# Hybrid decoder step on one core: the y products of eight heads in one burst, four buffers for the cumulative sums, a 4 KB DMA scratch

## The chip, the cores and the metric

The kernel runs on one core of a Trainium2 chip. The core has five engines with a queue each: TensorE (PE, matrix products), VectorE (DVE), ScalarE (ACT), GpSimd (POOL) and SyncE (SP, which here issues most DMAs). An engine works through its own queue in order; a wait at the head holds what is behind it. Sixteen DMA engines serve all queues. The metric is the device time of one execution in microseconds.

## The reference

One layer of a hybrid decoder on 256 prompt tokens and 8 x 8 sample tokens (320 in all), model width 2048, float32:

```python
h = rms_norm(x, p["norm_mix_pre"])
proj = h @ p["w_in"]                       # gate u, v; z; x, B, C; dt
gate_out, chunk_v = chunk_spatial_gate(a_u, a_v, ...)
ssm_out, new_ssm, new_ssm_conv = ssd_mixer(z, xbc, dt_raw, ...)
mix = jnp.concatenate([gate_out, ssm_out], axis=-1) @ p["w_out"]
x = x + rms_norm(mix, p["norm_mix_post"])
f, new_ffn_conv = conv_ffn(rms_norm(x, p["norm_ffn_pre"]), ...)
x = x + rms_norm(f, p["norm_ffn_post"])
```

The change lies in the chunked scan of `ssd_mixer`, which has 32 heads in 4 groups:

```python
seg = da_cs[:, :, :, None] - da_cs[:, :, None, :]
decay = jnp.exp(jnp.where(mask, seg, -jnp.inf))
cb = jnp.einsum("bctgn,bcsgn->bctsg", cc, bc)
y_diag = jnp.einsum("bctsgr,bcsgrp->bctgrp", cb[..., None] * decay, xdt)
...
y_off = jnp.einsum("bctgn,bcgrpn,bctgr->bctgrp", cc, states_in, jnp.exp(da_cs))
```

`da_cs` are the cumulative sums of dt times a. For each head the decay matrix is made from them, multiplied by `cb`, and then multiplied with the inputs of that head: that is the y product.

## The kernel before

All 320 tokens are kept as columns. A weight matrix comes in slabs of 128 x 1024 values: `slab` (L118) asks for one through SP into a `wraw` buffer (three of them), ACT casts it to a high part `whi` (L128), and DVE subtracts to get the low part `wlo` (L130); each of these has three buffers too. `accumulate` (L139) then runs three products of 128 x 128 weights on 128 x 320 columns (L141, L142, L143): high x high, high x low, low x high. A slab holds eight such weight blocks, so 24 products. `project` (L166) computes 512 output columns of a projection that way, `chunk_out` (L222) adds 512 rows of an output projection to `acc`.

Work that is not weight products is written as generators ("tasks") in the list `bg`; `tick` (L154) runs the first task to its next `yield`. `project` and `chunk_out` call `tick` after a slab, once or `rate` times, so the number of `yield`s sets how far along the weight stream a step stands in program order. That is not the final order: at the end a scheduler places every engine's instructions by priority (program order, moved by `high_priority` and `issue_after`) and by when it thinks their inputs and buffers are there, and can pull a ready instruction ahead of its place.

The scan of a group is the task `ssd(g)` (L767). In order: transposes of x to token order (`xt_ps`), state loads, the loads of the cumulative sums (`load_sums`, L780: two heads' sums, broadcast to 128 partitions, 320 KB, into a `cs` buffer), the chunk's state (`s1_ps`), `cb` (`cb_ps`) and the sample states' part (`yo_ps`). Then for each head `decays(hl)` (L874). For the first head of a pair: ACT takes the exponential of the sums (L880) into `cpx`, POOL multiplies by C (L881). For every head: DVE subtracts (L887, three instructions), ACT takes the exponential (L889), DVE multiplies by `cb` (L891), all in place in `cs`. `products(j)` (L894) runs the products of a pair of heads into one PSUM tile `y_ps` (L902) and DVE adds the skip term into `xs` (L912). After all of them POOL scales the state (L924), `final()` (L927) multiplies the last state product (`fin_ps`, L929) and DVE adds it (L931). The small PSUM tiles (`misc`, L57: `y_ps`, `fin_ps`, `xt_ps`, `cb_ps` and others) share a pool of four banks.

Before, the loads of three pairs are asked for together (L830), and `decays` and `products` run in two halves of four heads (L915 to L923); the fourth pair's sums are asked for behind the first half's products, when a `cs` buffer has been read.

`heads_out(g)` (L944) projects z for the group, and its evacuation `z_evac` (L949) multiplies silu(z) into y (`ev` L359 by DVE, silu L360 by ACT), so it needs that group's y. The stream around the four groups is `chunk_out(w_out, 3)`, then for each group the z projection, the next x projection and `chunk_out(w_out, 4 + g)`, with two ticks a slab in most of them (L980 to L999).

[...]

Of the kernel before, what the change touches and what calls it, by code (L numbers as in the profile page):

```python
# [9 lines left out]
F32 = mybir.dt.float32  # L10
# [7 lines left out]
P = 128  # L18
# [3 lines left out]
NT = NP + NS  # L22
# [12 lines left out]
def hybrid_step(  # L35
# [9 lines left out]
    nc = tc.nc  # L45
# [6 lines left out]
    wp = ctx.enter_context(tc.tile_pool(name="wp", bufs=3))  # L52
# [4 lines left out]
    def misc(name):  # L57
        return ms.tile([P, 512], F32, tag="ms", name=name)
# [54 lines left out]
    def turn():  # L113
        return tc.issue_after(in_turn[-1]) if in_turn else nullcontext()

    first_raw = []

    def slab(src):  # L118
        n = src.shape[2]
        with tc.high_priority(offset=100000):  # L120
            m = n * src.shape[1]
            raw = wp.tile([P, 1024], F32, tag="wraw", name="wraw", bufs=3) if len(first_raw) < 2 else first_raw.pop(0)
            with turn() if first_raw else nullcontext():
                slab_load.append(sp.dma_start(raw[:, :m].rearrange("p (a n) -> p a n", n=n), src).ins)
            if first_raw:
                in_turn.append(slab_load[-1])
            hi = wp.tile([P, 1024], F32R, tag="whi", name="whi", bufs=3)
            act.copy(hi[:, :m], raw[:, :m])  # L128
            lo = wp.tile([P, 1024], F32R, tag="wlo", name="wlo", bufs=3)
            dve.tensor_tensor(out=lo[:, :m], in0=raw[:, :m], in1=hi[:, :m].bitcast(F32), op=ALU.subtract)  # L130

        def block(k, c):
            o = k * n + c * P
            return hi[:, o:o + P], lo[:, o:o + P]
        return block
# [30 lines left out]
    def project(w, c0, evac, width=512, late=None, before=None, quiet=0, ready=None, small=0, after=None, ahead=1, rate=1, more=None, held=None):  # L166
# [6 lines left out]
        def part(src, k0, nk, js):  # L173
            wb = slab(src)
            for c, j in enumerate(js):
                for k in range(nk):
                    kt = k0 + k
                    accumulate(ps[j][:, :NT], wb(k, c), hT[0][:, kt, :], hT[1][:, kt, :], kt == 0, kt == KD - 1)
                if kt == KD - 1 and late is None:
                    if before and j in (0, 2):  # L180
                        before()
                    if before and j == 2:
                        for i in range(2):
                            evac(i, ps[i])
                    if not before or j > 1:
                        evac(j, ps[j])
            if k0 < KD - quiet:
                for _ in range(rate):
                    tick()
# [32 lines left out]
    def chunk_out(w, ck, hi, lo, begins, done=None, rate=1):  # L222

        for nb in range(KD):
            if nb % 2 == 0:
                wb = slab(rows_of(w, 4 * ck, 4, P * nb, 256))
            ps = mm.tile([P, 512], F32, tag="mm", name=f"pd_{ck}_{nb}")
            for k in range(4):
                made = accumulate(ps[:, :NT], wb(k, nb % 2), hi[:, k, :], lo[:, k, :], k == 0, k == 3)
            with first():  # L230
                if begins:
                    act.copy(acc[:, nb, :], ps[:, :NT])
                else:
                    dve.tensor_tensor(out=acc[:, nb, :], in0=acc[:, nb, :], in1=ps[:, :NT], op=ALU.add)  # L234
            if done is not None:
                done(nb)
            if nb % 2 == 1:
                for _ in range(rate):
                    tick()
        pd_last.append(made)  # L240
# [141 lines left out]
    def by_head(ap):  # L382
        return ap.rearrange("p (h d) -> p h d", d=64)
# [7 lines left out]
    with ExitStack() as mctx:  # L391
# [350 lines left out]
        with tc.tile_pool(name="sd", bufs=1) as sd:  # L742
# [24 lines left out]
            def ssd(g):  # L767
# [11 lines left out]

                def load_sums(j):  # L780

                    cs = sd.tile([P, 2, NT], F32, tag="cs", name="cs", bufs=3)
                    o = NS * (j // 2)
                    sp.dma_start(cs, dacs_d[h0 + 2 * j:h0 + 2 * j + 2, o:o + NT].unsqueeze(0).broadcast_to([P, 2, NT]))
                    return cs
# [31 lines left out]
                def decayed(i, c):  # L817
                    xde = sd.tile([P, 512], F32, tag="xde", name="xde", bufs=1)
                    pool.tensor_tensor(out=by_head(xde), in0=by_head(xdt[:, c, :]),
                                      in1=dec[:, i, h0:h0 + 8].unsqueeze(2).to_broadcast([P, 8, 64]), op=ALU.mult)  # L820
                    return xde
# [5 lines left out]
                                      op=ALU.mult)  # L827
                sts.append(load_state(3))
                yield from repeat(None, 5)
                sums_of = {j: load_sums(j) for j in range(3)}  # L830
                yield
                ps = misc("s1_ps")
                pe.matmul(ps, btok[:, 0, bs], x0d, start=True, stop=True)
# [36 lines left out]
                def places(hl):  # L870

                    return ((NS, P), (NS + P, P), (0, NS)) if hl < 4 else ((0, P), (P, P), (NP, NS))

                def decays(hl):  # L874
                    j, i = hl // 2, hl % 2
                    at = places(hl)
                    if i == 0:
                        cs = sums_of.pop(j)
                        cpx = sd.tile([P, 2, P], F32, tag="cpx", name="cpx", bufs=2)
                        act.activation(cpx, cs[:, :, at[1][0]:at[1][0] + P], AF.Exp)  # L880
                        pool.tensor_tensor(out=cpx, in0=cpx, in1=cT[:, g, P:2 * P].unsqueeze(1).to_broadcast([P, 2, P]),  # L881
                                           op=ALU.mult)
                    else:
                        cs, cpx = made[hl - 1][1:]
                    m = cs[:, i]
                    for c, (o, n) in enumerate(at):
                        dve.tensor_scalar(out=m[:, o:o + n], in0=m[:, o:o + n], scalar1=nda[:, c, h0 + hl:h0 + hl + 1],  # L887
                                          scalar2=0.0, op0=ALU.add, op1=ALU.min)
                    act.activation(m, m, AF.Exp)  # L889
                    o = NS * (hl // 4)  # L890
                    dve.tensor_tensor(out=m, in0=m, in1=cb[:, o:o + NT], op=ALU.mult)  # L891
                    made[hl] = m, cs, cpx

                def products(j):  # L894

                    ps = misc("y_ps")
                    pair = [(i, *made[2 * j + i]) for i in range(2)]

                    def both(cols, w, x, **flags):
                        for i, m, _, cpx in pair:  # L900
                            hl = 2 * j + i
                            pe.matmul(ps[64 * i:64 * i + 64, cols], w(hl), x(hl, m, cpx), tile_position=(0, 64 * i), **flags)  # L902

                    def hs(hl):
                        return slice(64 * hl, 64 * hl + 64)
                    c0, c1, sm = (slice(o, o + n) for o, n in places(2 * j))
                    both(slice(0, P), lambda hl: xdt[:, 0, hs(hl)], lambda hl, m, cpx: m[:, c0], start=True, stop=True)
                    both(slice(P, NP), lambda hl: xdt[:, 1, hs(hl)], lambda hl, m, cpx: m[:, c1], start=True, stop=False)
                    both(slice(P, NP), lambda hl: s1[:, hs(hl)], lambda hl, m, cpx: cpx[:, hl % 2, :], start=False, stop=True)
                    both(slice(NP, NT), lambda hl: xdt[:, 2, hs(hl)], lambda hl, m, cpx: m[:, sm], start=True, stop=True)  # L910
                    y = xs[:, j, :]
                    dve.scalar_tensor_tensor(out=y, in0=y, scalar=d_col[:, 4 * g + j:4 * g + j + 1], in1=ps[:, :NT],  # L912
                                             op0=ALU.mult, op1=ALU.add)
                x1d = decayed(1, 1)
                for j in range(0, 4, 2):  # L915
                    for hl in range(2 * j, 2 * j + 4):
                        decays(hl)
                        yield
                    yield
                    products(j)  # L920
                    products(j + 1)
                    if j == 0:
                        sums_of[3] = load_sums(3)  # L923
                pool.tensor_tensor(out=by_head(s1), in0=by_head(s1),  # L924
                                   in1=dec[:, 2, h0:h0 + 8].unsqueeze(2).to_broadcast([P, 8, 64]), op=ALU.mult)

# [9 lines left out]
                else:  # L936
                    for _ in final():
                        pass
                    yield

            tasks = [ssd(g) for g in range(4)]
            res = [[] for _ in range(4)]

# [439 lines left out]
```

## Time and profile before

| | us |
|---|---|
| median of 3 runs | 1777.94 (1777.39 to 1778.95) |
| the profiled execution | 1777.77 |
| its span | 1775.7 |
| PE busy in the span | 1766.8 |
| weight load (PEld) busy | 1743.1 |
| DVE busy | 1184.3 |
| ACT busy | 798.8 |
| POOL busy | 273.2 |

The span is the time from the first to the last instruction of the profiled execution; 2.1 us of its time lie around it. Busy times are sums over instructions; matmuls are pipelined, so neighbouring ones overlap in the record and a busy PE can still lose time between two kinds of product. In a row of instructions in time, the columns are start, duration, engine, line, operation, output and inputs, shapes, count, and in brackets the idle time before it and what ended it. The four groups' scans lie between about 430 and 720 us, the FFN from about 820 us on.

### The profile page before, as it was taken

The numbers are of one execution on the slowest core, as the hardware profiler recorded it, in microseconds if no ns is written. First come the engines' busy times: TensorE is split into PE (matmuls) and PEld (weight loads), VectorE is DVE, ScalarE is ACT, GpSimd is POOL, SyncE is SP. The second block draws the span as 40 slices with busy tenths as digits, with TensorE's granted clock in tenths as the row PEclk, the third lists the DMA queues.
The fourth block names the chain that finished last, engine by engine and source line by source line (L and its number), as shares of the span: only waits on it lengthen the run. The fifth ranks groups of instructions, "written<-read, shape, count | busy, mean of one in ns | idle before, by whom it ended". The sixth has DMA issues, their size and how long they took to land.

```text
span 1775.7 us, 31251 instructions
## 1 busy us (share of the span) xinstructions
PE 1766.8 (100%) x12234; PEld 1743.1 (98%) x12234; DVE 1184.3 (67%) x2055; ACT 798.8 (45%) x1108; POOL 273.2 (15%) x591
## 2 busy tenths in 40 slices
PE   9999999999999999999999999999999999999998
PEld 9999999999999899999999999999999999999998
DVE  7348854656877778577966666766666575656475
ACT  7344544333545454445645434343434343433335
POOL 2003210000211101012322212021101010101004
PEclk9999999999999999999999999999999999999999
DMA  7455644445664644444556656566554444444442
GB/s 253 136 165 167 196 151 149 155 154 192 214 211 156 193 161 148 155 161 155 161 189 199 208 174 206 181 197 204 178 194 147 153 150 151 157 146 153 152 149 107
DMA packets 228498, 303.04 MB, mean 171 GB/s; under 512 B 19488, under 2 KB 150656, under 8 KB 228160
## 3 DMA queue, kind: packets, MB, share of 16 engines
q1 hardware_dynamic: 216560, 281.27, 49.5%
q10 hardware_dynamic: 10304, 15.30, 2.4%
q0 software_dynamic: 1488, 4.49, 0.8%
q8 instruction: 96, 1.57, 0.3%
q14 instruction: 50, 0.41, 0.1%
HBM read 283.44 MB, written 17.58 MB: 170 GB/s over the span
## 4 chain that ended last, share of the span: by engine, by line
PE 96%; DVE 1%; DMA 1%; ACT 1%; issue 0%; POOL 0%; SPq 0%; DVEq 0%; ACTq 0%; POOLq 0%
PE ps L141 20%; PE ps L143 20%; PE ps L142 20%; PE pd L141 10%; PE pd L142 10%; PE pd L143 10%; PE y_ps L902 1%; DMA cs<-dacs_d 1%; PE sg L708 0%; PE yo_ps L851 0%; PE up_ps L1197 0%; DMA wraw<-in_w_in 0%; PE tsum L282 0%; PE vt_ps L597 0%; PE xt_ps L380 0%
## 5 line engine op out<-in xcount | busy, mean ns | idle before, releaser
L130 DVE TENSOR_TENSOR wlo<-wraw,whi 128x1024 fp32r<-128x1024 f32 x470 | 584.6, 1244 | 384.7 <-ACT whi L128 382.0
L128 ACT CAST whi<-wraw 128x1024 fp32r<-128x1024 f32 x470 | 492.1, 1048 | 706.1 <-PE ps L142 413.4
L141 PE MATMUL ps<-h_hi,whi 128*128 128x320 f32 x2528 | 783.2, 310 | 1.3 <-DVE ev L359 0.9
L142 PE MATMUL ps<-h_lo,whi 128*128 128x320 f32 x2528 | 780.1, 309 | 0.0
L143 PE MATMUL ps<-h_hi,wlo 128*128 128x320 f32 x2528 | 779.7, 309 | 0.2 <-DVE wlo L130 0.2
L141 PEld LDWEIGHTS ps<-h_hi,whi 128*128 128x128 f32 x2528 | 474.8, 188 | 4.2 <-issue 1.8
L142 PEld LDWEIGHTS ps<-h_lo,whi 128*128 128x128 f32 x2528 | 474.9, 188 | 1.2 <-issue 0.5
L143 PEld LDWEIGHTS ps<-h_hi,wlo 128*128 128x128 f32 x2528 | 474.4, 188 | 0.6 <-DVE wlo L130 0.5
L141 PE MATMUL pd<-fhi,whi 128*128 128x320 f32 x704 | 217.3, 309 | 0.0
L143 PE MATMUL pd<-fhi,wlo 128*128 128x320 f32 x704 | 217.3, 309 | 0.0
L142 PE MATMUL pd<-flo,whi 128*128 128x320 f32 x704 | 217.3, 309 | 0.0
L141 PE MATMUL pd<-ohi,whi 128*128 128x320 f32 x448 | 139.1, 311 | 0.0
L142 PE MATMUL pd<-olo,whi 128*128 128x320 f32 x448 | 139.0, 310 | 0.0
L143 PE MATMUL pd<-ohi,wlo 128*128 128x320 f32 x448 | 138.7, 310 | 0.0
L142 PEld LDWEIGHTS pd<-flo,whi 128*128 128x128 f32 x704 | 132.2, 188 | 0.7
L143 PEld LDWEIGHTS pd<-fhi,wlo 128*128 128x128 f32 x704 | 132.2, 188 | 0.0
L141 PEld LDWEIGHTS pd<-fhi,whi 128*128 128x128 f32 x704 | 132.2, 188 | 0.0
L234 DVE TENSOR_TENSOR acc_ffn<-acc_ffn,pd 128x320 f32<-128x320 f32 x160 | 77.2, 483 | 33.3 <-PE pd L143 32.4
L141 PEld LDWEIGHTS pd<-ohi,whi 128*128 128x128 f32 x448 | 84.1, 188 | 1.0 <-issue 0.4
L142 PEld LDWEIGHTS pd<-olo,whi 128*128 128x128 f32 x448 | 84.1, 188 | 0.7 <-issue 0.4
L143 PEld LDWEIGHTS pd<-ohi,wlo 128*128 128x128 f32 x448 | 84.1, 188 | 0.2 <-issue 0.2
L1094 POOL COPY ptf<-pad 128x2 f32<-128x2 f32 x88 | 19.8, 227 | 405.2 <-DVE pad L1082 404.6
(300 smaller groups left out, 1578.6 us busy)
## 6 DMA issues: line engine op xcount, KB each, us to landing
wraw<-in_ffn_w_up SPq DMA_DIRECT2D x176, 512.0 KB, 3.5
wraw<-in_w_in SPq DMA_DIRECT2D x142, 512.0 KB, 3.5
wraw<-in_ffn_w_down SPq DMA_DIRECT2D x88, 512.0 KB, 3.3
wraw<-in_w_out SPq DMA_DIRECT2D x64, 512.0 KB, 3.3
st<-in_state_ssm SPq DMA_DIRECT2D x64, 256.0 KB, 4.3
out_ssm_state_sample<-st ACTq DMA_DIRECT2D x32, 256.0 KB, 2.6
cs<-dacs_d SPq DMA_DIRECT2D x16, 320.0 KB, 4.9
xr<-in_xT SPq DMA_DIRECT2D x4, 640.0 KB, 4.6
```

The costliest lines, as they stand in the source:

```text
L128: act.copy(hi[:, :m], raw[:, :m])
L130: dve.tensor_tensor(out=lo[:, :m], in0=raw[:, :m], in1=hi[:, :m].bitcast(F32), op=ALU.subtract)
L141: pe.matmul(ps, whi, xhi, start=first, stop=False)
L142: pe.matmul(ps, whi, xlo, start=False, stop=False)
L143: newest[0] = pe.matmul(ps, wlo, xhi, start=False, stop=last).ins
L234: dve.tensor_tensor(out=acc[:, nb, :], in0=acc[:, nb, :], in1=ps[:, :NT], op=ALU.add)
L902: pe.matmul(ps[64 * i:64 * i + 64, cols], w(hl), x(hl, m, cpx), tile_position=(0, 64 * i), **flags)
L1094: pool.tensor_copy(ptf[:, k, :], pad[:, 256:258])
```

## The change

The task asks for all four pairs' sums together, into four `cs` buffers in place of three; it runs the decays of all eight heads, and then the products of all four pairs in one go. One `yield` a group falls away. `cpx` has four buffers in place of two and `wraw` four in place of three. [...]

```diff
-            raw = wp.tile([P, 1024], F32, tag="wraw", name="wraw", bufs=3) if len(first_raw) < 2 else first_raw.pop(0)
+            raw = wp.tile([P, 1024], F32, tag="wraw", name="wraw", bufs=4) if len(first_raw) < 2 else first_raw.pop(0)
...
-                    cs = sd.tile([P, 2, NT], F32, tag="cs", name="cs", bufs=3)
+                    cs = sd.tile([P, 2, NT], F32, tag="cs", name="cs", bufs=4)
...
-                sums_of = {j: load_sums(j) for j in range(3)}
+                sums_of = {j: load_sums(j) for j in range(4)}
...
-                        cpx = sd.tile([P, 2, P], F32, tag="cpx", name="cpx", bufs=2)
+                        cpx = sd.tile([P, 2, P], F32, tag="cpx", name="cpx", bufs=4)
...
-                for j in range(0, 4, 2):
-                    for hl in range(2 * j, 2 * j + 4):
-                        decays(hl)
-                        yield
+                for hl in range(8):
+                    decays(hl)
                     yield
+                yield
+                for j in range(4):
                     products(j)
-                    products(j + 1)
-                    if j == 0:
-                        sums_of[3] = load_sums(3)
...
-    nc = _bacc.Bacc("TRN2", target_bir_lowering=False, num_devices=1)
+    nc = _bacc.Bacc("TRN2", target_bir_lowering=False, num_devices=1, dynamic_dma_scratch_size=4096)
```

## The prediction

> **What bounds the kernel now.** I read the page's first lines and the chain that ended last, then the busy time by stage, then the order of TensorE's (PE's) instructions around the products of y.
>
> ```profile
> span 1775.7 us, 31251 instructions
> PE 1766.8 (100%) x12234; PEld 1743.1 (98%) x12234; DVE 1184.3 (67%) x2055; ACT 798.8 (45%) x1108; POOL 273.2 (15%) x591
> PE 96%; DVE 1%; DMA 1%; ACT 1%; issue 0%; POOL 0%; SPq 0%; DVEq 0%; ACTq 0%; POOLq 0%
> ...
> 500.00:600.00 100.00, 99.58 (x741) 93.57 (x740) 78.20 (x153) 49.29 (x71) 12.60 (x25) 1.00 0.54 175
> 600.00:720.00 120.00, 118.15 (x888) 113.11 (x889) 85.24 (x170) 54.95 (x79) 13.69 (x20) 1.00 0.51 164
> 830.00:1700.00 870.00, 870.00 (x5917) 868.61 (x5916) 567.00 (x919) 369.76 (x485) 145.04 (x378) 1.00 0.54 174
> ...
> 5.53 6.31 DMA wraw<-in_w_in
> ...
> 813.88 1.23 DVE wlo L130
> ```
>
> The columns of the stage rows are: stretch, its length, then busy time and instructions of PE, weight load, DVE, ACT, POOL, the granted clock, the DMA share and GB/s. The last two rows are of the chain of waits: start, length, what. PE is idle for 1775.7 - 1766.8 = 8.9 us. Of these 0.4 + 1.9 = 2.3 us lie between 500 and 720 us, in the stage of the four ssd groups; nearly all the rest is the start and the tail, where the changed code doesn't run. From 830 to 1700 PE has no gap, so deeper weight loading (the fourth `wraw` buffer) has nothing to win there. What is left is in 436 to 720 us: the idle time, and time in which PE counts as busy while it changes from one kind of product to another.
>
> **The price of a change of kind.** Two full bursts of group 0 and the broken ones of group 1:
>
> ```profile
> 477.49 0.31 PE L143 MATMUL pd<-ohi,wlo 128*128 128x320 f32 x1
> 477.73 0.66 PE L902 MATMUL y_ps<-cs,xdt 128*64 128x128 f32 x8
> ...
> 479.42 0.42 PE L141 MATMUL pd<-ohi,whi 128*128 128x320 f32 x1
> 479.67 0.31 PE L142 MATMUL pd<-olo,whi 128*128 128x320 f32 x1
> ...
> 489.94 0.31 PE L143 MATMUL pd<-ohi,wlo 128*128 128x320 f32 x1
> 490.18 0.66 PE L902 MATMUL y_ps<-cs,xdt 128*64 128x128 f32 x8
> ...
> 492.98 0.31 PE L142 MATMUL ps<-h_lo,whi 128*128 128x320 f32 x1
> ...
> 558.48 0.31 PE L141 MATMUL pd<-ohi,whi 128*128 128x320 f32 x1
> 558.72 0.43 PE L902 MATMUL y_ps<-cs,xdt 128*64 128x128 f32 x2
> 559.08 0.42 PE L142 MATMUL pd<-olo,whi 128*128 128x320 f32 x1
> 559.34 0.31 PE L143 MATMUL pd<-ohi,wlo 128*128 128x320 f32 x1
> ...
> 559.87 0.54 PE L902 MATMUL y_ps<-cs,xdt 128*64 128x128 f32 x5
> ...
> 575.69 0.43 PE L902 MATMUL y_ps<-cs,xdt 128*64 128x128 f32 x2
> ...
> 576.31 0.31 PE L141 MATMUL pd<-ohi,whi 128*128 128x320 f32 x1
> 576.54 0.54 PE L902 MATMUL y_ps<-cs,xdt 128*64 128x128 f32 x5
> ...
> 577.71 0.31 PE L143 MATMUL pd<-ohi,wlo 128*128 128x320 f32 x1
> ...
> 580.50 0.31 PE L141 MATMUL pd<-ohi,whi 128*128 128x320 f32 x1
> 580.74 0.43 PE L902 MATMUL y_ps<-cs,xdt 128*64 128x128 f32 x2
> 581.10 1.12 PE L929 MATMUL fin_ps<-xde,btok 128*128 128x512 f32 x2
> ...
> 585.01 0.63 PE L380 MATMUL xt_ps<-ident,x 128*128 128x128 f32 x4 [0.42 <-DVE s L931]
> ...
> 585.63 0.31 PE L143 MATMUL pd<-ohi,wlo 128*128 128x320 f32 x1
> ```
>
> Weight products start 0.147 us apart (870 / 5917). A `products(j)` leaves 16 records. From the last weight product before the burst to the second one after it, less two steps of 0.147: 32 records cost 479.67 - 477.49 - 0.29 = 1.89 us; two records cost 559.34 - 558.48 - 0.29 = 0.57; the fourteen between 576.31 and 577.71 (16 less the two at 575.69) cost 1.40 - 0.29 = 1.11. That is about 0.044 us a record and 0.48 us for each entry and exit together, a *join*. The start gaps alone give the lower bound: 0.24 in and 0.25 out against 0.147 each, 0.2 us. I take 0.4, nearer the fit.
>
> **The change, part by part.**
>
> *One burst in place of two.* Before, PE enters the products 11 times: twice in group 0, five times in group 1 (558.72, 559.87, 575.69, 576.54, 580.74), twice each in groups 2 and 3, as in group 0. After, the eight heads' decays come first and then all 64 records: 4 entries. The number of products is the same. 7 joins at 0.4 = 2.8 us less (bounds 7 x 0.2 = 1.4 and 7 x 0.48 = 3.4).
>
> *The transposes behind group 1's last burst.* From 580.50 to 585.63 PE spends 5.13 - 0.29 = 4.84 us on 16 records (0.7), the state product `fin_ps`, 16 transposes and a join (0.4). `fin_ps` is worth 492.98 - 489.94 - 0.29 - 1.89 = 0.86 us in group 0.
>
> ```profile
> 496.53 1.75 PE xt_ps L380 x16
> ```
>
> The transposes alone take 1.75. So 4.84 - 0.7 - 0.86 - 1.75 - 0.4 = 1.1 us is waiting: the last transposes want a PSUM bank that POOL L924 and DVE L931 must clear first. With group 1's burst two ticks earlier (one `yield` fewer in each of two groups) the transposes need no longer stand there, but then need a join of their own: -1.1 + 0.4 = -0.7 us (bounds -1.1 and 0).
>
> *Four buffers for the sums.* With three, the fourth pair's `cs` is asked for only once the first pair's is read, and SP, DVE and ACT wait for it in order:
>
> ```profile
> 611.65 1.14 SPq L784 DMA_DIRECT2D cs<-dacs_d  x2
> 621.30 1.36 SPq L784 DMA_DIRECT2D cs<-dacs_d  x2
> ...
> 621.27 0.54 PE L902 MATMUL y_ps<-cs,xdt 128*64 128x128 f32 x5 [0.49 <-DVE cs L891]
> ...
> 627.00 0.42 ACT L880 ACTIVATE cpx<-cs 128x256 f32<-128x256 f32 x1 [5.93 <-DMA cs<-dacs_d]
> ...
> 633.96 0.41 PE L141 MATMUL ps<-h_hi,whi 128*128 128x320 f32 x1 [0.93 <-DVE ev L359]
> ...
> 639.11 0.41 PE L143 MATMUL ps<-h_hi,wlo 128*128 128x320 f32 x1 [0.19 <-DVE wlo L130]
> ```
>
> The load at 611.65 is late for group 2's own products: 0.49 us of PE, gone after the change, since all four loads go out behind the previous group's burst, well ahead. The loads at 621.30 belong to group 3. ACT's exponential of them stands 5.9 us ahead of the casts and the silu of z, and PE pays 0.93 + 0.19 = 1.1 us. This wait remains in kind: four loads go out behind each burst and their exponentials may again stand too early in ACT's queue. It moves away from the end of the z projection by about three ticks, so I take half: -0.55 (bounds -1.1 and, as rival 2 works out, a large loss).
>
> *PSUM.* A burst now holds all four `ms` banks (the four-bank PSUM pool), and `fin_ps` needs the first back.
>
> ```profile
> L912 DVE SCALAR_TENSOR_TENSOR xs<-xs,prm,y_ps x16: 529/542/549, 478.8 to 711.0; 128x320 f32<-128x320 f32 x16
> ```
>
> The first y is ready after 0.4 / 2 + 0.7 = 0.9 us, its evacuation takes 0.54, and a weight split may stand ahead with 1.2 (the row at 813.88): free at 2.7 us, while the burst lasts 0.4 + 64 x 0.044 = 3.2. Cost zero, hidden by the other three products. [...]
>
> *New pieces.* The instruction order is found by a scheduler, which broke two of the eight old bursts apart. By that share one of the four new ones breaks: +0.45 us (bounds 0 and 4, +1.8).
>
> *`cpx` buffers, `wraw` buffer, scratch.* Four `cpx` tiles go with the four `cs`. The fourth `wraw` lets SP ask one slab (24 products of 0.147, 3.5 us of PE) earlier; the splits stay at three buffers, and PE waits for a load only at the start, for the slab issued at 5.53 us, which has its buffer already: 0 (bounds +-1.2, one weight split, since the chain's row at 813.88 is such a split at the turn to the FFN, and it may be placed otherwise). [...]
>
> **Sum**, against the profiled execution's 1777.77 us (span 1775.7 and 2.1 around it; median 1777.94): -2.8 - 0.7 - 0.5 - 0.55 + 0.45 = -4.1, so **1773.7 us**. All gains at their bounds and no new piece: -3.4 - 1.1 - 0.5 - 1.1 = -6.1, 1771.7.
>
> **Rivals.** (1) *The bursts stay broken.* The products of a pair are ready as soon as its own decays are, so the scheduler may again slip them singly between weight products, as at 558.72 and 575.69. Then the joins stay, and only the waits go: -0.5 - 0.7 = -1.2, 1776.6. Against it: the first three pairs' decays now lie well ahead of the burst in program order.
> (2) *Slower: ACT waits on four sums.* Two loads outstanding kept ACT 5.9 us. Two more are 655 KB, 2.9 us at the 226 GB/s of 436 to 500 us:
>
> ```profile
> 436.00:500.00 64.00, 64.00 (x495) 61.27 (x494) 54.79 (x121) 32.30 (x51) 14.03 (x25) 1.00 0.68 226
> ```
>
> Three split slabs cover 3 x 3.5 us less a cast and a split (1.0 + 1.2), so 8.3 us. At 639.11 the cover was spent with 5.9, since z's work stood in the same queues. If it is spent behind each of three bursts, 2.9 us a time is 8.7: 1777.8 - 2.8 + 8.7 = 1783.7. It decides from a wait of about 6 us beside a z evacuation, 8.3 elsewhere. Against it: groups 0 and 1 had such waits without loss to PE.
> (3) *`fin_ps` waits for its bank*, because DVE stands at a `cs` load (taken as 2.5 us, half of ACT's 5.9 at 627.00, since half of it is past) when y comes: 2.7 + 2.5 - 3.2 = 2.0 us at three groups, +6.0 less 4.1: 1779.7.
>
> **How the numbers follow.** The forecast .60, its own range 1771.7 to 1775.6 (three more pieces, 1.35, and the z wait kept, 0.55); rival 1 .16, rival 2 .16, rival 3 .08. A measurement of this kernel tells about 0.2%, 3.6 us, from no change: below 1774.4 is faster, above 1781.5 slower. Of the forecast's .60, .44 lie below 1774.4; its rest, rival 1 and rival 3 are within, .40; rival 2 is slower, .16. The range 1771.5 to 1781.5 leaves out rival 2 and little else.
>
> **What would show it.** Right: four entries to `y_ps` with 64 records each, 3.2 us long, the state product right behind; no PE wait on `cs`; 500 to 720 us with under 1 us of idle PE; the rest of the trace unmoved. Wrong: `y_ps` records in small groups (rival 1); ACT or DVE idle over 8 us on `cs<-dacs_d` and PE waiting for `whi` or `wlo` behind a burst (2); PE waiting for L912 (3); a new gap at the start or at 810 to 825 us would be the fourth `wraw`.

## The result and the profile after

The changed kernel takes 1775.87 us (median of 12 runs, 1773.68 to 1779.46) beside 1779.06 us for the kernel before on the same chip (12 runs, 1776.73 to 1781.03): ratio 0.9984, 95% interval 0.9976 to 0.9991. Run a second time, against another set of the kernel before, it gave 0.9994 (0.9985 to 1.0003). So the gain is 0.06 to 0.16%, 1 to 3 us, and within the 0.2% that counts as no change. Of 4.1 us forecast, a part came and a part was given back.

The profiled execution of the changed kernel took 1779.46 us, the slowest of its twelve. Its page, its stage rows (columns as in the prediction), and the four bursts in the chain of waits (start, length, what; group 1's burst is in the next view):

```profile
span 1777.7 us, 31251 instructions
PE 1766.5 (99%) x12234; PEld 1743.3 (98%) x12234; DVE 1184.2 (67%) x2055; ACT 790.1 (44%) x1102; POOL 278.9 (16%) x591
...
180.00:190.00 10.00, 9.79 (x56) 9.79 (x57) 10.00 (x23) 4.41 (x5) 3.76 (x7) 0.83 0.79 264
436.00:500.00 64.00, 62.76 (x485) 59.67 (x484) 54.53 (x115) 32.65 (x54) 10.60 (x24) 1.00 0.73 238
500.00:600.00 100.00, 98.98 (x739) 94.73 (x741) 81.77 (x169) 50.41 (x79) 15.45 (x28) 1.00 0.54 178
600.00:720.00 120.00, 119.49 (x922) 114.84 (x915) 83.73 (x164) 49.62 (x71) 11.02 (x18) 1.00 0.51 162
...
491.20 3.18 PE y_ps L902 x63
...
619.07 3.24 PE y_ps L902 x64
...
705.51 3.24 PE y_ps L902 x64
```

PE's idle time between 500 and 720 us fell from 2.3 to 1.0 + 0.5 = 1.5 us. Where before had none, 436 to 500 us, there are now 1.2 us, and at 180 to 190 us the granted clock is 0.83 where it was 1.00. The burst of group 1, in order of PE's instructions:

```profile
572.66 0.31 PE L143 MATMUL pd<-ohi,wlo 128*128 128x320 f32 x1
572.90 0.66 PE L902 MATMUL y_ps<-cs,xdt 128*64 128x128 f32 x8
...
575.92 0.28 PE L902 MATMUL y_ps<-cs,xdt 128*64 128x64 f32 x4
576.14 0.41 PE L141 MATMUL pd<-ohi,whi 128*128 128x320 f32 x1
576.39 0.31 PE L142 MATMUL pd<-olo,whi 128*128 128x320 f32 x1
...
576.98 1.02 PE L926 MATMUL fin_ps<-xde,btok 128*128 128x512 f32 x2
...
581.87 0.76 PE L380 MATMUL xt_ps<-ident,xs 128*128 128x128 f32 x5 [0.76 <-ACT xs L424]
```

All four bursts are whole, 64 records in 3.2 us. By the prediction's reckoning this one costs 576.39 - 572.66 - 0.29 = 3.44 us, where two bursts of 32 cost 2 x 1.89 = 3.78: a join is worth 0.34.

For all kernels of this study, the lengths of seven stages of each one's profiled execution, between the first starts of certain PE products (us; *rows*: last `vt_ps` transposes L597 to `dt_ps` L468, the stage in which the late gate norm rows arrive; *enter*: last `sg` L708 to group 0's first `s_ps` L833; *g0*: from there to the first token sums L282 behind its burst; *g1+2*, *g3*: between the following token sums; *tail*: from the token sums at the mixer's end, 814.46 us in before, to the next ones, 864.04 us, by when the FFN's weights are already running; *FFN*: from there to the token sums at its end, 1759.55 us). The pieces between these stages differ by at most about 0.9 us from kernel to kernel. The kernels below "after" are the experiments.

| kernel | rows | enter | g0 | g1+2 | g3 | tail | FFN | span |
|---|---|---|---|---|---|---|---|---|
| before | 71.72 | 41.74 | 77.02 | 105.50 | 88.86 | 49.59 | 895.50 | 1775.7 |
| after | 75.92 | 43.63 | 77.20 | 101.39 | 88.54 | 48.98 | 896.04 | 1777.7 |
| a_again | 72.07 | 43.27 | 78.15 | 101.42 | 88.53 | 49.27 | 896.13 | 1774.5 |
| e_halves | 73.90 | 42.93 | 78.86 | 102.67 | 88.92 | 48.45 | 896.26 | 1777.8 |
| e_wraw3 | 71.75 | 43.94 | 78.39 | 101.31 | 88.52 | 49.87 | 895.50 | 1775.9 |
| e_scratch | 71.71 | 41.84 | 77.03 | 105.80 | 88.87 | 50.20 | 895.50 | 1776.8 |
| e_bwraw4 | 73.18 | 42.26 | 77.02 | 105.74 | 88.86 | 48.73 | 896.98 | 1779.1 |
| b_rows | 71.71 | 41.62 | 77.02 | 105.74 | 88.89 | 49.83 | 895.52 | 1775.8 |
| e_first | 72.29 | 41.62 | 77.22 | 102.02 | 88.52 | 49.57 | 895.73 | 1772.8 |
| e_rows | 71.71 | 43.14 | 77.41 | 102.06 | 88.53 | 48.93 | 895.91 | 1773.2 |
| e_best | 71.71 | 41.62 | 76.67 | 101.61 | 88.54 | 48.44 | 896.08 | 1770.5 |
| e_best_again | 71.74 | 41.62 | 76.68 | 102.32 | 88.54 | 49.15 | 896.81 | 1772.4 |
| e_best_w3 | 71.71 | 41.62 | 76.68 | 101.79 | 88.52 | 48.59 | 895.50 | 1770.5 |

A gain of 4.1 us is there in g1+2, and one of 0.3 in g3. Against it stand *enter* (+1.9), *g0* and *rows* (+4.2 in this execution).

**Loss 1, entering group 0.** The rows of SP, DVE, POOL and PE in the kernel after,

```profile
441.65 3.73 SPq L784 DMA_DIRECT2D cs<-dacs_d  x3
...
450.01 2.07 DVE L887 TENSOR_SCALAR cs<-cs,nda 128x128 f32<-128x128 f32 x7 [2.39 <-DMA cs<-dacs_d]
...
453.13 3.51 DVE L887 TENSOR_SCALAR cs<-cs,nda 128x64 f32<-128x64 f32 x10
...
457.70 1.43 DVE L887 TENSOR_SCALAR cs<-cs,nda 128x128 f32<-128x128 f32 x7
...
453.53 2.15 POOL L881 TENSOR_TENSOR cpx<-cpx,cT 128x256 f32<-128x256 f32 x3 [2.28 <-ACT cpx L880]
...
462.13 0.39 PE L141 MATMUL pd<-ohi,whi 128*128 128x320 f32 x1 [0.78 <-DVE pad L413]
```

and DVE's rows of the kernel before at the same place:

```profile
445.61 2.07 DVE L887 TENSOR_SCALAR cs<-cs,nda 128x128 f32<-128x128 f32 x7 [2.48 <-DMA cs<-dacs_d]
...
448.74 1.89 DVE L887 TENSOR_SCALAR cs<-cs,nda 128x64 f32<-128x64 f32 x7
...
451.68 0.47 DVE L887 TENSOR_SCALAR cs<-cs,nda 128x128 f32<-128x128 f32 x2
```

The sums are asked for from 441.65 us on, behind state loads in SP's queue, and arrive at 450. DVE waits for them no longer than before (2.39 and 2.48 us). What has grown is the work behind the wait: 7 + 10 + 7 = 24 subtractions, 7.0 us, in place of 7 + 7 + 2 = 16, 4.4 us. A pair has six subtractions. The eight that are new here are the fourth pair's six and two of the third pair's, which in before came at 480.82 us, behind ACT's exponential L880 at 480.04: that exponential writes a third `cpx` tile, and before has two buffers for it. So `cpx` has a part in this loss as well as `cs`. The eight by themselves are about 1.6 us. The other 1.0 us is that four of the 24 in place of two of the 16 take 0.74 to 0.87 us instead of 0.24 to 0.29; each of them lies beside one of POOL's multiplications L881, of which the row above shows three. All this now stands between weight splits and ahead of the evacuations `pad` L412 and L413, which PE needs. PE stops twice for them:

```profile
PE pd L141 <- DVE pad L413: 1.1, 2, 0.8
PE xt_ps L380 <- ACT xs L424: 0.8, 1, 0.8
PE ps L141 <- DVE acc_mix L234: 0.3, 1, 0.3
```

(Total us, times, longest, of PE's waits from 430 to 600 us.) **Loss 2, behind group 0's burst.** Group 1's subtractions, and DVE's wait for their loads, stand ahead of the evacuation `acc_mix` L234. DVE and PE in a_again, where this costs more:

```profile
493.00 0.45 DVE L887 TENSOR_SCALAR cs<-cs,nda 128x128 f32<-128x128 f32 x2 [2.36 <-DMA cs<-dacs_d]
...
494.79 1.42 DVE L887 TENSOR_SCALAR cs<-cs,nda 128x128 f32<-128x128 f32 x4 [0.38 <-ACT cpx L880]
...
496.52 2.19 DVE L887 TENSOR_SCALAR cs<-cs,nda 128x128 f32<-128x128 f32 x6
498.63 0.47 DVE L234 TENSOR_TENSOR acc_mix<-acc_mix,pd 128x320 f32<-128x320 f32 x1
...
497.64 0.31 PE L143 MATMUL ps<-h_hi,wlo 128*128 128x320 f32 x1
499.16 0.41 PE L141 MATMUL ps<-h_hi,whi 128*128 128x320 f32 x1 [1.21 <-DVE acc_mix L234]
```

The step from 497.64 to 499.16 is 1.52 us in place of 0.15. In the kernel before, the last of these evacuations began at 492.34 us. Only four of group 1's subtractions stood among them (489.54 to 492.42 us, without a wait for a load), and DVE's wait came behind them and was shorter:

```profile
496.70 0.28 DVE L887 TENSOR_SCALAR cs<-cs,nda 128x128 f32<-128x128 f32 x1 [0.80 <-DMA cs<-dacs_d]
```

The loads of the sums take a median of 6.6 us from issue to landing in after and 4.9 in before. PE's loss goes with DVE's wait for them: 0.3 to 0.5 us of PE at 1.4 to 1.7 us of DVE (after, e_rows, e_first), 1.2 at 2.4 (a_again), 1.5 at 3.0 (e_wraw3).

**Loss 3, the late norm rows.** POOL, DVE and PE in the kernel after:

```profile
165.44 6.92 POOL L625 COPY v_there<-bT 128x1 f32<-128x1 f32 x1
...
174.10 1.06 POOL L667 DMA_DIRECT2D lb<-in_gate_ln_b  x2
...
171.57 1.41 DVE L675 SCALAR_TENSOR_TENSOR vt<-vt,rs_r,lb 128x512 f32<-128x512 f32 x2
178.27 0.75 DVE L675 SCALAR_TENSOR_TENSOR vt<-vt,rs_r,lb 128x512 f32<-128x512 f32 x1 [5.29 <-DMA lb<-in_gate_ln_b]
...
178.17 0.31 PE L142 MATMUL ps<-h_lo,whi 128*128 128x320 f32 x1
180.21 0.42 PE L143 MATMUL ps<-h_hi,wlo 128*128 128x320 f32 x1 [1.74 <-DVE wlo L130]
```

and POOL and DVE in the kernel before:

```profile
159.85 0.53 POOL L625 COPY v_there<-bT 128x1 f32<-128x1 f32 x1
...
165.49 5.78 POOL L410 COPY pad<-sst 128x24 f32<-128x24 f32 x1
171.21 0.54 POOL L667 DMA_DIRECT2D lb<-in_gate_ln_b  x1
...
174.93 0.75 DVE L675 SCALAR_TENSOR_TENSOR vt<-vt,rs_r,lb 128x512 f32<-128x512 f32 x1 [3.07 <-DMA lb<-in_gate_ln_b]
```

A copy of 128x1 that took 0.53 us in before took 6.92 here; DVE was at work beside both. The loads of `lb`, issued by POOL behind it, leave 2.9 us later; DVE waits for them with a weight split behind it, and PE with DVE: 5.29 us where 3.07 cost PE nothing. None of the scan's changed lines runs here, but the weight loads with their fourth buffer do, and the program is built with the scratch of 4096 bytes.

### The profile page after: what moved, and what is told of

Its sections match the earlier page's. It is cut to its first block, busy times and chain, and to the rows that moved or that the text cites. A ratio compares the mean times of both kernels' runs of the same rounds, so it can differ in the third digit from the quotient of the medians.

```text
span 1777.7 us, 31251 instructions
## 1 busy us (share of the span) xinstructions
PE 1766.5 (99%) x12234; PEld 1743.3 (98%) x12234; DVE 1184.2 (67%) x2055; ACT 790.1 (44%) x1102; POOL 278.9 (16%) x591
## 4 chain that ended last, share of the span: by engine, by line
PE 93%; DVE 3%; DMA 2%; issue 1%; ACT 1%; POOL 1%; SPq 0%; DVEq 0%; ACTq 0%; POOLq 0%
PE ps L141 20%; PE ps L143 19%; PE ps L142 19%; PE pd L141 10%; PE pd L143 10%; PE pd L142 10%; DVE wlo L130 1%; DMA cs<-dacs_d 1%; PE y_ps L902 1%; DVE cs L887 0%; PE sg L708 0%; PE yo_ps L851 0%; PE up_ps L1194 0%; DVE cv L419 0%; PE tsum L282 0%
## 5 line engine op out<-in xcount | busy, mean ns | idle before, releaser
L234 DVE TENSOR_TENSOR acc_ffn<-acc_ffn,pd 128x320 f32<-128x320 f32 x160 | 77.2, 483 | 33.3 <-PE pd L143 32.3
```

## The experiments

**a_again**: the changed kernel once more, no edit.

> The changed kernel once more. Two theories on its profiled execution, which took 1779.46 us where the median is 1775.87. Theory L (late rows): POOL's copies ran long while DVE was busy without a pause (6.92 us for one copy at 165.4), the layer norm's row lb was asked for late, DVE stood 5.3 us before it with weight splits behind, and PE lost about 4 us before 210 us; it comes and goes with timing. Then a second profile has dt_ps at 205 to 206 us where POOL was not held up, and the span is shorter by what that stretch is shorter. Theory M: the changed kernel always loses it (fourth weight buffer or scratch): dt_ps again near 210. Both: 0.1 to 0.25% under the kernel before; four bursts of 64 y records; PE idle in 436 to 500 us near 1.2 us, since group 0's sums land late.

1777.12 us (11 runs, 1774.88 to 1779.78), ratio 0.9994 (0.9985 to 1.0003). *Rows* is back at 72.07: loss 3 comes and goes with the execution. Losses 1 and 2 stay (+1.5 and +1.1).

**e_halves**: the products in two halves as before, with the sums still asked for together.

```diff
-                for hl in range(8):
-                    decays(hl)
-                    yield
-                yield
-                for j in range(4):
+                for j in range(0, 4, 2):
+                    for hl in range(2 * j, 2 * j + 4):
+                        decays(hl)
+                        yield
+                    yield
                     products(j)
+                    products(j + 1)
```

> The changed kernel with the products again in two halves of four heads; sums, cpx and weight buffers and the scratch stay as changed. Theory J (the joins carry the gain): 4 joins come back at 0.4 us, more if the scheduler breaks the halves up: 1.6 to 2.8 us slower than the changed kernel, about 1 us under the kernel before. Rival S (the sums asked for together carry it): within 0.5 us of the changed kernel, no PE wait on cs.

1779.03 us (1776.39 to 1781.12), ratio 1.0002 (0.9993 to 1.0011): no gain over before is left, though the interval overlaps a_again's. In g3, where nothing else differs, the halves cost 88.92 - 88.53 = 0.39 us. In g1+2, 2.8 of the 4.1 us stay, so asking early is worth 2.8 there and the single burst 1.25. Most of the 1.25 is not joins: around z's evacuation PE's steps from one weight product to the next, less 0.147 us each, add up to 1.80 us here against 0.95 in a_again. The idle part of it is 0.9 us for `ev` L359 and 0.2 for `wlo` between 600 and 720 us, as before, against 0.5 and none in a_again (totals of PE's waits in e_halves):

```profile
PE ps L141 <- DVE ev L359: 0.9, 1, 0.9
...
PE ps L143 <- DVE wlo L130: 0.2, 1, 0.2
```

So both theories have a part. Behind group 0's second half PE also waits 0.6 us for `whi` and 0.7 for `wlo` (512.83 and 514.09 us), the sign of rival 2, in *g0* of 78.86 us.

Beside z's evacuation of group 2, at 628 to 642 us, ACT has four `ACT_TABLE_LOAD` rows of 1.28 us in before and two in after; between 430 and 720 us there are 15 and 10. That fits the shorter wait at z (0.9 us for `ev` L359 in before, 0.3 in after), but it was not tried by itself.

**e_wraw3** (changed kernel, `wraw` with `bufs=3`), **e_scratch** (kernel before with the scratch of 4096 bytes alone) and **e_bwraw4** (kernel before with the scratch and `wraw` with `bufs=4`):

> The changed kernel with three weight load buffers, as before the change. My reading (no PE wait on a load after the start): within 1 us of the changed kernel. Rival B (the fourth buffer carries the gain): 2 to 3 us slower, back at the time before.

> The kernel before with the scratch of 4 KB alone. My reading: same order of instructions, same time within 0.05%. [...]

> The kernel before with four weight load buffers and the scratch of 4 KB, nothing else. My reading: no gain, within 0.05% of the kernel before; the four stretches of the ssd groups as before (41.7, 77.0, 105.5, 88.9 us). Rival (deeper loading delays the row loads and sums): the stretch from vt to dt_ps over 72 us, up to 0.1% slower. Rival (deeper loading carries the gain): 2 us faster.

Ratios 0.9994 (0.9985 to 1.0003), 1.0 (0.9991 to 1.0009) and 1.0003 (0.9994 to 1.0012). The scratch by itself changes nothing. The fourth `wraw` gains nothing in the whole time. In e_bwraw4 *rows* takes 73.18 us, over the 72 that was named as the sign of row loads delayed by deeper loading, and the FFN stage is 1.5 us longer, with these rows of ACT, DVE and PE:

```profile
1226.57 0.62 ACT L1181 CAST xsp<-raw 128x512 fp32r<-128x512 f32 x1 [3.76 <-DMA raw<-xq_d]
...
1227.22 0.69 DVE L1182 TENSOR_TENSOR xsp<-raw,xsp 64x512 fp32r<-64x512 f32 x1 [2.94 <-ACT xsp L1181]
...
1228.49 0.41 PE L141 MATMUL ps<-h_hi,whi 128*128 128x320 f32 x1 [0.68 <-DVE acc_ffn L234]
```

ACT and DVE stand at a late load, with the evacuation that PE waits for (L234) behind them. In before ACT waits 3.26 us at this place, and PE has no gap behind it.

**e_first**, against loss 1: group 0's sums are asked for ahead of its state loads, and its decays are put behind the last of its `xdt` products in the order (later groups as in the changed kernel).

```diff
+                sums_of = {j: load_sums(j) for j in range(4)} if g == 0 else {}
...
-                    dve.tensor_tensor(out=by_head(out), in0=by_head(ps),
+                    behind_x[0] = dve.tensor_tensor(out=by_head(out), in0=by_head(ps),
...
-                sums_of = {j: load_sums(j) for j in range(4)}
+                sums_of = sums_of or {j: load_sums(j) for j in range(4)}
...
-                    decays(hl)
+                    with tc.issue_after(behind_x[0]) if g == 0 else nullcontext():
+                        decays(hl)
```

> The changed kernel with group 0's four sums loads ahead of its state loads, and group 0's decays placed behind its xdt products on DVE. The stretch from the last sg product to the first state product took 41.7 us in the kernel before, 43.3 to 43.9 in three profiles of the changed form. Theory G (the four sums of group 0 land late, 8.3 us behind eight state loads, and hold DVE and ACT with weight splits behind): that stretch comes back to 41.7 to 42.2 us, total 1.5 us under the changed kernel. Rival D (DVE is simply full there: 24 subtractions moved into it): still over 43 us, total as the changed kernel.

1774.91 us (11 runs, 1773.04 to 1776.58), ratio 0.9982 (0.9973 to 0.9990). *Enter* is 41.62, as short as in any kernel. The rows of DVE:

```profile
444.14 2.15 DVE L889 TENSOR_SCALAR cs<-cs,nda 128x128 f32<-128x128 f32 x11
...
447.35 1.20 DVE L889 TENSOR_SCALAR cs<-cs,nda 128x64 f32<-128x64 f32 x6
...
449.59 1.36 DVE L889 TENSOR_SCALAR cs<-cs,nda 128x64 f32<-128x64 f32 x7
...
453.46 0.42 DVE L412 TENSOR_TENSOR pad<-ps,r 128x256 f32<-128x256 f32 x1
```

The subtractions (L889 here) begin without a wait at 444 and the last ends at 450.9, 2.5 us before `pad`. PE's wait for `pad` is gone. The 24 take 4.7 us here in place of 7.0: POOL's four multiplications were done at 443.0 us, and none of the 24 is stretched. How much of the cure is this, and how much the earlier loads and the place behind `xdt`, the run does not separate.

**e_rows** (changed kernel) and **b_rows** (kernel before), against loss 3: ACT's queue issues the late half of the norm row loads, so no POOL copy stands ahead of them.

```diff
-                            pool.dma_start(rows[-1], src[0:1, cs].broadcast_to([P, 512]))
+                            (act if q > 1 else pool).dma_start(rows[-1], src[0:1, cs].broadcast_to([P, 512]))
```

> The changed kernel with the late half of the layer norm's row loads issued by ACT in place of POOL. Theory L (in some executions POOL's stretched copies delay these loads and cost PE up to 4 us): the stretch from the last vt transposes to dt_ps, 71.7 us at best and 75.9 and 73.9 in two profiles, is 71.5 to 72; median 0.5 to 2 us under the changed kernel and a narrower spread. Rival: the spread of 4 to 5 us between executions comes from elsewhere; median and spread stay.

> The kernel before with only the late half of the layer-norm row loads issued by ACT instead of POOL. Theory L (those loads fall, in some executions, behind stretched POOL copies, in before as well as after): 0.5 to 1.5 us under before, a narrower spread than before's 4 to 5 us, stage vt to dt 71.7. Rival (only the changed kernel suffers, since its SP queue runs earlier): median within 0.3 us of before, spread as before's.

e_rows: 1775.9 us (1774.25 to 1777.74), ratio 0.9986 (0.9977 to 0.9995), 1.2 us under a_again. b_rows: 1777.32 us, ratio 0.9993 (0.9984 to 1.0001), with 11 runs from 1776.36 to 1777.88 where the kernel before had 1776.32 to 1780.74 beside it. By these medians before gains 1.0 us from the edit, but the interval reaches 1.0001, and no profile shows loss 3 in a kernel with three `wraw` buffers. Of the eight profiles in which POOL issues the late rows, the three with three buffers have *rows* of 71.71 to 71.75 us, and the five with four have 72.07 to 75.92; PE waits in three of these five (after, e_halves, e_bwraw4). In e_rows DVE's wait for `lb` is short:

```profile
172.41 0.75 DVE L675 SCALAR_TENSOR_TENSOR vt<-vt,rs_r,lb 128x512 f32<-128x512 f32 x1 [0.66 <-DMA lb<-in_gate_ln_b]
```

**e_best**: e_first, e_rows, and against loss 2 group 1's decays put behind its `cb` evacuation (L860).

```diff
-                dve.tensor_tensor(out=cb[:NS, NT:], in0=ps_cb[:NS, NP:NT], in1=upper_s[:NS], op=ALU.mult)
+                cb_done = dve.tensor_tensor(out=cb[:NS, NT:], in0=ps_cb[:NS, NP:NT], in1=upper_s[:NS], op=ALU.mult).ins
...
+                    with tc.issue_after(behind_x[0] if g == 0 else cb_done) if g < 2 else nullcontext():
```

> e_first and e_rows together, and group 1's decays placed behind its own cb evacuation. In the changed form PE lost 0.4 to 1.6 us at 500 us, where DVE and ACT stood at group 1's sums ahead of an evacuation; theory W says that goes (stretch from the first state product to the first token sums 76.5 to 77.0 us against 77.2 to 78.4), so with the others 3 to 4 us under the changed kernel, 0.25 to 0.35% under the kernel before. Rival: DVE runs out of time between cb and the burst, or other waits come in place: within 1 us of the changed kernel.

1772.72 us (6 runs, 1772.07 to 1774.89), ratio 0.9970 (0.9959 to 0.9982): faster than the kernel before, and 3.2 and 4.4 us under the two medians of the changed kernel. Between 436 and 500 us PE has no idle time left, and DVE evacuates without subtractions ahead:

```profile
436.00:500.00 64.00, 64.00 (x498) 61.65 (x497) 52.24 (x108) 31.48 (x49) 15.33 (x28) 1.00 0.71 226
...
491.12 0.49 DVE L234 TENSOR_TENSOR acc_mix<-acc_mix,pd 128x320 f32<-128x320 f32 x1 [1.01 <-PE pd L143]
```

*g0* is now 76.67, 0.35 under before: with the wait away, one join saved shows there as it does in g3.

**e_best_again** (no edit) and **e_best_w3** (`wraw` with `bufs=3`):

> The same kernel as e_best, a second time, beside the two below. If its gain of 0.30% over before is real: 0.25 to 0.35% under before, median 1771.5 to 1774.0 us, stages as in e_best's profile: 71.7 (vt transposes to dt), 41.6 (last sg to the first state product of group 0), 76.7 (from there to the first token sums), 101.6 (groups 1 and 2). If the first value came from few runs by luck: 0.1 to 0.2% under before, as the changed kernel itself.

> e_best with three buffers for the raw weights. The stage from the FFN's start to its last product was 895.50 us in each of the three profiled kernels with three such buffers and 895.7 to 897.0 in the six with four, but the stage ahead of it was 0.6 us shorter on average with four. Theory N (the fourth buffer is worth nothing): within 0.05% of e_best_again. Rival F (the fourth buffer costs the FFN its 0.2 to 1.5 us): FFN stage 895.5 and a median 0.5 to 1.5 us under e_best_again. Rival H (it helps the rest, which is then read off the sum): 1 to 2 us over.

1772.69 us (ratio 0.9971, 0.9961 to 0.9982) and 1772.1 us (0.9967, 0.9954 to 0.9979). The gain holds. Over all profiles the FFN stage is 895.50 to 895.52 in the five with three `wraw` buffers and 895.73 to 896.98 in the eight with four. The medians 0.6 us apart fit that (rival F), but their intervals overlap: the price is shown in the stage, not in the whole time. The *tail* stage ahead of it is shorter with four, 48.9 us on average against 49.6, so that over both stages the two forms differ by less than 0.1 us on average.

## Why the prediction was only partly right

- **One burst, joins.** Right in kind: four entries of 64 records, 3.2 us. The join taken at 0.4 measured 0.32 to 0.40 (g3 in five kernels with halves against eight with one burst: 88.86 to 88.92 and 88.52 to 88.54), nearer the fit (0.48) than the gaps (0.2). In group 1, where 48 records in four entries and 16 more by the prediction's own price cost 4.13 + 1.10 us and now 3.44, a join is worth 0.45. With 0.35 in group 0 (e_best), 0.34 in group 2 (e_halves against after) and 0.32 in group 3, the seven joins give the 2.8 us that were forecast. No burst broke; the +0.45 for a new piece didn't come as such, but in group 1 `fin_ps` and the transposes now stand apart, with joins of their own.
- **Group 1's transposes, the fourth pair, the z evacuation.** Together with five joins the forecast for g1+2 was 5 x 0.4 + 0.7 + 0.5 + 0.55 = 3.75 us; it measured 4.1, so the sum was near. The terms were not, and that they make up for each other is luck. The transposes' -0.7 hardly came. From 580.50 to 585.63 us PE was idle 0.42 us and not 1.1; the rest was further changes of kind, since the 14 products behind `fin_ps` (582.15 us) are a twelfth entry that the count of 11 leaves out. By the prediction's reckoning `fin_ps` and the transposes cost 3.74 us there; after the change they cost 3.46 (a_again) and 3.84 (after), with a wait for ACT's `xs` L424 of 0.4 and 0.8 us. The late load was worth more than the 0.49 us of idle: group 2's second half with its `fin_ps` takes 3.66 us of PE in before and 2.74 in e_halves, 0.92 less. Around z PE lost 1.70 us in before by its steps, 0.54 in after and 0.95 in a_again: 0.75 to 1.16 less where 0.55 was taken.
- **PSUM at nothing.** Right: PE has no wait on L912, and in groups 0 and 2 `fin_ps` follows the burst directly. Rivals 1 and 3 did not occur in the changed kernel.
- **`wraw`, `cpx`, scratch at nothing.** Right for the whole time: the scratch, which has no term in the sum, is 0 (e_scratch, ratio 1.0), and the fourth `wraw` loses 0.2 to 1.5 us in the FFN stage, in one profile more than the bound of 1.2, and wins about as much in *tail*. `cpx` was not tried by itself; with two buffers, two of the eight subtractions of loss 1 would by the order before have stayed behind, which no run shows.
- **The step that failed** is the term of the fourth pair's sums. It counted what goes (the late load, -0.5) and not what moves with it. At the entry to group 0 that is eight subtractions of DVE, moved to a place ahead of PE's evacuations: 2.6 us of DVE, 1.0 of it from subtractions beside POOL's work. Rival 2 was about the right place in the order, but priced the length of ACT's wait and found for its own rejection that "groups 0 and 1 had such waits without loss to PE". At the entry the wait did not grow; the work queued behind it on DVE did. Behind group 0's burst the wait did grow, as rival 2 said, from 0.80 to between 1.4 and 3.0 us, but on DVE, and what PE missed was an evacuation and not a weight split. a_again loses 1.5 us in *enter*, and in *g0* 1.1 although a join is saved there (1.5 without it). e_first and e_best show it from the other side: with the same 24 subtractions begun earlier, or group 1's placed behind the evacuations, the loss goes and the gain stays.
- **"The rest of the trace unmoved"** failed too. The *rows* stage took 75.92 and 72.07 us in two executions of the changed kernel, and made the profiled execution of the change slower than that of before in spite of its gain. Without it, the tally from before to a_again is -4.1 - 0.3 in the y stages, +1.5 + 1.1 at the two places of losses 1 and 2, +0.3 in the tail and FFN together, +0.3 in *rows*: -1.2, the difference of the spans (1775.7 and 1774.5).

The forecast's 1773.7 us would have been about right with these two places in order: e_best gains 0.30%, 5.3 us, of which some 1 us is the norm rows, if the medians of b_rows and before are taken at their word.

What stays open: why PE has a gap behind the load of `xq_d` in e_bwraw4, where ACT waits 3.76 us for it, and none in before, where it waits 3.26, and whether the bad case of *rows* needs the fourth `wraw`. It came in three of five profiles with four buffers and in none of three with three, which is too few to tell.

## What to carry to other kernels

When loads are asked for together, their readers move with them (here eight subtractions, and 2.6 us of DVE at the entry to group 0): count those instructions on every engine, and look whose evacuation they now stand ahead of. A wait that was harmless before is harmless only for the work that stood behind it then (here a wait of DVE of 2.48 us went with no wait of PE in before, and one of 2.39 us with 1.1 us of PE in after). Before comparing two profiles, compare stages that the change isn't meant to touch: here one of them moved by 4.2 us, more than the whole effect.

## What the hardware showed that was not expected

- POOL's long copies of Loss 3 end close to the end of a run of DVE without a pause: in the kernel after the 6.92 us copy (L625) ends at 172.4 us and DVE's run at 173.0, in the kernel before the 5.78 us copy (L410) ends at 171.3 us and DVE's run at 171.9. But the copy of L625 took 0.53 us at 159.85 in the kernel before, beside DVE's L419, which also runs beside the long copies; what decides between the two is not shown here.
- A step of 2.04 us between two products (1.74 of it idle) was followed by products 0.27 us apart in place of 0.147, until 184 us. The granted clock was 0.60 from 180.00 to 184.30 us and 1.00 from there to 190. In e_halves a step of 1.84 us at the same place, 1.53 of it idle, was followed by products 0.147 us apart, and the granted clock was 1.00 from 180 to 190 us. The kernel after:

```profile
180.61 0.44 PE L142 MATMUL ps<-h_lo,whi 128*128 128x320 f32 x1
...
184.05 0.31 PE L143 MATMUL ps<-h_hi,wlo 128*128 128x320 f32 x1
```

So the step cost 1.9 us by itself, and the slower products behind it 1.5 us more (13 steps from 180.61 to 184.05, 3.44 us in place of 13 x 0.147 = 1.91). These are two steps 0.2 us apart in length, one with a lower clock behind it and one without; what lowered it is not shown.
